# Down projections of three feed-forwards written as seven-product pairs, in four parts instead of three

## The chip, the cores and the metric

The kernel runs on one core of one Trainium2 chip. The metric is the device time of one launch in microseconds (us); the number given for a kernel is the median of its runs. Five engines work side by side, each through its own queue of instructions in order: PE (TensorE: matrix products from SBUF into the eight banks of PSUM), DVE (VectorE), ACT (ScalarE), POOL (GpSimd) and SP (SyncE, which here only issues transfers). POOL also issues transfers, among them all that add to what lies at their destination. An engine waits for another by semaphores.

## The reference, cut to what matters

One step of a streaming encoder of two layers over 512 prompt frames and 64 sample frames, 576 columns in all, with a model width of 1024. Every layer has two feed-forwards, four in the whole, each added with a half:

```
def swiglu(x, w_gu, w_down):
    gate, up = jnp.split(x @ w_gu, 2, axis=-1)
    return (jax.nn.silu(gate) * up) @ w_down
...
x = x + 0.5 * swiglu(rms_norm(x, ln_ffn1[l]), w_ffn1_gu[l], w_ffn1_down[l])
```

The hidden width is 2816, which is 22 tiles of 128. `x @ w_gu` is the gate-up projection, the product with `w_down` the down projection. Between the feed-forwards stand attention, a short convolution, a state space layer and cross attention, which the change leaves alone.

## The kernel before, in words

The activations lie transposed: `X` holds the residual as 8 row tiles (numbered `f`) of 128 x 576. All products are made to nearly fp32 precision from two terms: an operand is split into a high part (`wh`, `xh`, `hh`, rounded by ACT, `hi`) and a low part (`wl`, `xl`, `hl`, the difference, by DVE, `lo`), and a product takes three passes, high by high, high by low and low by high. The 576 columns are two halves of 288 (`HF`), `one` and `two`, so that a product of one 128 x 128 weight tile with all columns costs 6 matmuls of 288 columns.

Three of the four feed-forwards (the second of layer 0, both of layer 1) have `pairs` set. There the gate-up projection goes tile by tile, each hidden tile with its gate and its up weights as one `Pair`: two output tiles, two halves of the inner dimension (4 row tiles each) and two halves of the columns form a 2 x 2 by 2 x 2 product, computed with seven products instead of eight (Strassen's scheme in Winograd's form). A product is 4 row tiles by three passes, 12 matmuls of 288 columns, so a pair is 84 matmuls. Its price lies elsewhere:

* Sums of weights. A pair loads its two weight tiles by SP into `wraw` (`r1`) and `raw2` (`r2`), and `pair_ahead` and `pair_sums` make the four sums that the products need: three transfers issued by POOL that add to their destination (L292 into `raw2`, L300 into `wraw` from DRAM, L302 into `wraw` from `ss`) and one addition on DVE (L299, `ss`). L300 may start only when `ss` has been made and product 0's weights have been split, L302 only when product 2's weights have been split, and product 5's weights (`r1`, second half) exist only when L302 has landed. L292 belongs to the pair after.
* Splits. Each product's weights are split on their own, 128 x 512: one ACT instruction, then one DVE instruction.
* Sums of results. `pair_epi` combines the products, which accumulate in three PSUM banks `T`, `Y`, `W` of the pair (products 0, 3, 4, 6 in `T`; 1 and 5 in `Y`; 2 in `W`); two pairs in turn use six banks. It ends with the hidden tile `td` and its split into `hh` and `hl`.

The order is written out by hand. `pair_steps` sorts the products by `7 * n + at[k]`: a pair's products go 0, 1, 2, 3, then product 6 of the pair before, then 5, 4. `run_steps` emits, ahead of the step in hand, the splits of weights up to four products further on, then the matmuls, then the pair's epilogue, then what was deferred. Since each engine runs its queue in order, on DVE the split of product 5 stands ahead of the splits of product 4 and of the next pair's 0, 1 and 2.

The 22 hidden tiles go in `PARTS` of 6, 8 and 8. After the gate-up pairs of a part (`pair_steps` is called once a part; in its last pair the order is 5, 4, 6 with nothing between), the part's down projection runs in eight steps `down`, one for each `f`: `nj` weight tiles of 6 matmuls each into two PSUM banks, weights loaded and split whole (128 x 768 or 128 x 1024). In the first two parts two DVE instructions (L664, L665) scale the sum by the row statistics `R` and add it to `X`; in the last part `R` has been put into `td` before (L608), and one instruction (L661) adds to `X`. In that part `finalize` follows for each `f`: it prepares the next stage's operands. Where the next stage is again a feed-forward in pairs (after the second feed-forward of layer 0) this is `finalize_s` with its sums and differences `eh`, `el`; after the third one, where the output follows, the last part's down runs as `down_two` and `down_final` in column blocks of 320 and 256.

Of the kernel before, what the change touches and what calls it, by code (L numbers as in the profile page):

```python
# [17 lines left out]
KT = 8  # L18
# [5 lines left out]
NJ = 22  # L24
PARTS = ((0, 6), (6, 8), (14, 8))
PAIRED = (0, 4, 1, 5, 2, 6, 3, 7)
PAST = 256
# [22 lines left out]
class Part:  # L50


    def __init__(self, pair, k):
        self.pair, self.k = pair, k
# [16 lines left out]
class Pair:  # L71

    def __init__(self, g1, g2):
        self.g = (g1, g2)
        self.kw = g1.shape[1] // 2
        self.half = slice(0, self.kw), slice(self.kw, 2 * self.kw)


class Kernel:
# [39 lines left out]
    def operand(self, st):  # L121
        st["hh"] = self.hhl.tile([128, KT, NT], F32R, tag="hh", name="hh")
        st["hl"] = self.hhl.tile([128, KT, NT], F32R, tag="hl", name="hl")

# [178 lines left out]

    def pair_steps(self, grans, ops, epi, late):

        mm = self.nc.tensor.matmul
        todo = []
        for n, (g1, g2) in enumerate(grans):  # L310
            pr = Pair(g1, g2)
            pr.n = n
            pr.banks = [self.banks[:, 3 * (n % 2) + b, :HF] for b in range(3)]
            at = {0: 0, 1: 1, 2: 2, 3: 3, 5: 5, 4: 6, 6: 11}
            if late and n < 2:
                at = ({0: 0, 1: 1, 2: 4, 3: 6, 5: 7, 4: 9, 6: 12}, {0: -5, 1: -4, 2: -2, 3: 1, 5: 3, 4: 4, 6: 6})[n]
            elif n == len(grans) - 1:
                at = {0: 0, 1: 1, 2: 2, 3: 3, 5: 5, 4: 6, 6: 9}
            todo += [(7 * n + at[k], k, pr) for k in range(7)]

        def one(w, k, pr):
            out = pr.banks[PLACE[k]]
            xh, xl = ops()[k]
            for kk in range(4):
                ws = slice(kk * 128, kk * 128 + 128)
                for pi, (ww, xx) in enumerate(((w[0], xh), (w[0], xl), (w[1], xh))):
                    mm(out, ww[:, ws], xx[:, kk], start=k < 3 and kk == 0 and pi == 0, stop=kk == 3 and pi == 2,  # L327
                       skip_group_check=True)
            epi(k, pr)
# [207 lines left out]
    def ffn(self, gu, dn, gain_next, pairs=True, early=False):  # L537
# [3 lines left out]

        def pair_epi(k, pr, first, last, scaled):

            T, Y, W = pr.banks
            tt = V.tensor_tensor
            jj = pr.n
            one, two = slice(0, HF), slice(HF, NT)
            if k == 0:
                if jj == 0:
                    self.operand(st)  # L550
                pr.tb, pr.ta, pr.tc = (self.tmp(n) for n in ("tb", "ta", "tc"))
                self.hi(pr.tb[:, one], T)
# [30 lines left out]
            elif k == 4:  # L583
                tt(pr.tc[:, two], T, pr.tb[:, two], op=ALU.add)  # L584
            else:
                h = self.tmp("td")
                hh, hl = st["hh"][:, jj], st["hl"][:, jj]

                def rest():
                    self.lo(hl, h, hh)  # L590

                def tail():
                    self.hi(hh, h)
                    self.defer(rest, 1)

                if last:
                    for c, u in ((one, T), (two, pr.tc[:, two])):
                        tt(h[:, c], u, pr.ta[:, c], op=ALU.mult)
                        if scaled:
                            tt(h[:, c], h[:, c], st["R"][:, c], op=ALU.mult)  # L600
# [4 lines left out]
                tt(h[:, one], T, pr.ta[:, one], op=ALU.mult)  # L605
                tt(h[:, two], pr.tc[:, two], pr.ta[:, two], op=ALU.mult)
                if scaled:
# [4 lines left out]
        for pi, (j0, nj) in enumerate(PARTS):  # L612
            def lead(wg, wu):
# [55 lines left out]
            def down_mm(w, ps, c0, n, ks):  # L669
                for k in ks:  # L670
                    for pi, (ww, xx) in enumerate(((w[0], st["hh"]), (w[0], st["hl"]), (w[1], st["hh"]))):
                        nc.tensor.matmul(ps, ww[:, k * 128:(k + 1) * 128], xx[:, k, c0:c0 + n],  # L672
                                         start=k == 0 and pi == 0, stop=k == KT - 1 and pi == 2)

# [7 lines left out]
            def down_two(w0, w1, *part):  # L682
                c0, n, _ = part
                ps = [self.ps("ps_d")[:, 0, :n] for _ in range(2)]
                for ks in (range(KT - 1), (KT - 1,)):
                    for e, w in enumerate((w0, w1)):
                        down_mm(w, ps[e], c0, n, ks)
                for e, w in enumerate((w0, w1)):
                    st["w", e] = w
                    down_out(ps[e], e, *part)  # L690

            def down_final(w, f, *part):
                w = st.setdefault(("w", f), w)
                c0, n, _ = part
                ps = self.ps("ps_d")[:, 0, :n]
                down_mm(w, ps, c0, n, range(KT))
                down_out(ps, f, *part)

            if pairs:
                self.pair_steps([(gu[2 * j], gu[2 * j + 1]) for j in range(j0, j0 + nj)], ops,  # L700
                                lambda k, pr, j0=j0, nj=nj: pair_epi(k, pr, j0 + pr.n == 0, pr.n == nj - 1, j0 == PARTS[2][0]),
                                pi == 0)
            for jj in range(0 if pairs else nj):
# [5 lines left out]
                self.step(lambda w, jj=jj: up(w, jj), gu[2 * j + 1])  # L709
            if pairs and pi == 2 and not getattr(gain_next, "pairs", False):  # L710
                self.step(self.fs_close)
            if pi == 2 and gain_next is None:
                def dest(f):
# [17 lines left out]
            for i, f in enumerate(self.order(gain_next)):  # L731
                self.step(lambda w, f=f, nj=nj, la=(pi == 2), fi=(f == 0): down(w, f, nj, la, fi),
                          dn[f, :, j0 * 128:(j0 + nj) * 128])
                if pi == 2 and early and i == 0:
                    self.step(lambda: self.s5_open())
                elif pi == 2 and early and i in HALVES:
                    self.step(lambda *_: None, self.mem_half(1, HALVES.index(i)))
# [1548 lines left out]
def host_arrays(i):  # L2286
# [23 lines left out]
    for n in ("1", "2"):  # L2310
        out["gu" + n] = gu(f(f"w_ffn{n}_gu"))
        out["dn" + n] = np.stack([cols(w) for w in f(f"w_ffn{n}_down")])

    for n in ("xq", "xk", "xo"):
# [83 lines left out]
```

## Time and profile before

| | |
|---|---|
| median of 3 runs | 2562.05 us (2559.88 to 2564.67) |
| profiled execution, its own time | 2562.18 us |
| its span, first to last instruction | 2560.1 us |
| busy: PE, DVE, ACT, POOL | 97%, 64%, 42%, 20% of the span |
| mean granted clock of PE | 0.989 |
| first pair product of the three feed-forwards in pairs | 920 us, 1328 us, 2136 us after the start |

A profile row gives the start of a group, the time it took, the engine, the line of the program, the operation and its operands (output, arrow, inputs), and in brackets how long the engine had been idle before it and which instruction released it. Matmuls overlap, so the time from one start to the next counts, not the length of one.

### The profile page before, as it was taken

The numbers are of one execution on the slowest core, as the hardware profiler recorded it, in microseconds if no ns is written. First come the engines' busy times: TensorE is split into PE (matmuls) and PEld (weight loads), VectorE is DVE, ScalarE is ACT, GpSimd is POOL, SyncE is SP. The second block draws the span as 40 slices with busy tenths as digits, with TensorE's granted clock in tenths as the row PEclk, the third lists the DMA queues.
The fourth block names the chain that finished last, engine by engine and source line by source line (L and its number), as shares of the span: only waits on it lengthen the run. The fifth ranks groups of instructions, "written<-read, shape, count | busy, mean of one in ns | idle before, by whom it ended". The sixth has DMA issues, their size and how long they took to land. (4 is left out here: it accounts for less than half of the span.)

```text
span 2560.1 us, 45526 instructions
## 1 busy us (share of the span) xinstructions
PE 2477.1 (97%) x18499; PEld 2438.1 (95%) x18499; DVE 1628.7 (64%) x2762; ACT 1066.3 (42%) x1847; POOL 524.1 (20%) x667
## 2 busy tenths in 40 slices
PE   8999999999999999999999999999999999999998
PEld 8998999999899999999998999999999999999998
DVE  6645658567775675665776674755753467666574
ACT  5222222325654453443554352542453455344353
POOL 1476245202310010211101110212311001021111
PEclk9999999999999999999999999999999999999999
DMA  4465643321143354645545564745872225464551
GB/s 154 89 188 188 150 116 121 121 85 34 40 140 124 104 133 120 153 115 140 132 112 118 142 141 112 160 138 167 296 238 84 83 95 131 122 157 107 137 136 62
DMA packets 141074, 331.91 MB, mean 130 GB/s; under 512 B 19472, under 2 KB 48320, under 8 KB 140224
## 3 DMA queue, kind: packets, MB, share of 16 engines
q1 hardware_dynamic: 112352, 277.08, 33.8%
q0 software_dynamic: 28512, 51.92, 12.7%
q8 instruction: 145, 2.38, 0.4%
q14 instruction: 65, 0.53, 0.1%
HBM read 279.68 MB, written 31.97 MB: 122 GB/s over the span
## 5 line engine op out<-in xcount | busy, mean ns | idle before, releaser
L141 ACT ACTIVATE wh<-wraw 128x512 fp32r<-128x512 f32 (+2 forms) x543 | 430.3, 803 | 506.5 <-PE banks L406 229.7
L223 DVE TENSOR_TENSOR wl<-wraw,wh 128x1024 fp32r<-128x1024 f32 (+2 forms) x264 | 322.4, 1224 | 168.6 <-ACT wh L141 166.4
L406 PE MATMUL banks<-hh,wh 128*128 128x288 f32 x1768 | 382.4, 298 | 2.8 <-ACT hh L141 2.0
L406 PE MATMUL banks<-hh,wl 128*128 128x288 f32 x1768 | 380.5, 297 | 4.0 <-DVE wl L223 4.0
L406 PE MATMUL banks<-hl,wh 128*128 128x288 f32 x1768 | 380.9, 297 | 0.5 <-DVE hl L147 0.5
L327 PE MATMUL banks<-xh,wh 128*128 128x288 f32 x1056 | 312.0, 295 | 1.3 <-ACT tb L141 0.8
L327 PE MATMUL banks<-xh,wl 128*128 128x288 f32 x1056 | 311.4, 295 | 0.0
L327 PE MATMUL banks<-xl,wh 128*128 128x288 f32 x1056 | 310.9, 294 | 0.0
L406 PEld LDWEIGHTS banks<-hh,wh 128*128 128x128 f32 x1768 | 288.2, 191 | 4.4 <-ACT hh L141 2.5
L406 PEld LDWEIGHTS banks<-hh,wl 128*128 128x128 f32 x1768 | 287.1, 190 | 4.5 <-DVE wl L223 4.5
L406 PEld LDWEIGHTS banks<-hl,wh 128*128 128x128 f32 x1768 | 287.6, 191 | 1.0 <-DVE hl L147 1.0
L406 PE MATMUL banks<-xh,wh 128*128 128x288 f32 x1232 | 267.6, 299 | 10.0 <-ACT wh L141 9.1
L327 PE MATMUL banks<-eh,wh 128*128 128x288 f32 x792 | 238.8, 302 | 37.2 <-DVE tc L584 35.5
L147 DVE TENSOR_TENSOR wl<-wraw,wh 128x512 fp32r<-128x512 f32 x264 | 181.4, 688 | 144.9 <-ACT wh L141 131.7
L406 PE MATMUL banks<-xh,wl 128*128 128x288 f32 x1232 | 265.5, 297 | 5.3 <-DVE wl L223 5.3
L406 PE MATMUL banks<-xl,wh 128*128 128x288 f32 x1232 | 264.3, 296 | 0.0
L327 PE MATMUL banks<-el,wh 128*128 128x288 f32 x792 | 237.6, 300 | 0.0
L327 PE MATMUL banks<-eh,wl 128*128 128x288 f32 x792 | 237.3, 300 | 0.0
L406 PEld LDWEIGHTS banks<-xh,wh 128*128 128x128 f32 x1232 | 199.2, 190 | 12.2 <-ACT wh L141 9.6
L406 PEld LDWEIGHTS banks<-xh,wl 128*128 128x128 f32 x1232 | 199.0, 189 | 7.1 <-DVE wl L223 7.0
L327 PEld LDWEIGHTS banks<-xh,wh 128*128 128x128 f32 x1056 | 198.4, 188 | 2.6 <-DVE td L605 1.4
L406 PEld LDWEIGHTS banks<-xl,wh 128*128 128x128 f32 x1232 | 199.4, 190 | 0.0
(538 smaller groups left out, 4900.5 us busy)
## 6 DMA issues: line engine op xcount, KB each, us to landing
wraw<-in_gu SPq DMA_DIRECT2D x110, 512.0 KB
raw<-in_gu SPq DMA_DIRECT2D x66, 512.0 KB
wraw<-in_dn SPq DMA_DIRECT2D x64, 512.0 KB
raw<-in_gu POOLq DMA_DIRECT2D x66, 256.0 KB, 5.5
wraw<-in_gu POOLq DMA_DIRECT2D x66, 256.0 KB, 4.1
wraw<-ss POOLq DMA_DIRECT2D x66, 256.0 KB, 4.5
wraw<-in_dn SPq DMA_DIRECT2D x32, 384.0 KB
wraw<-in_win SPq DMA_DIRECT2D x17, 512.0 KB
```

What stands on the lines that cost most here:

```text
L141: self.nc.scalar.activation(out, in_, AF.Copy)
L147: self.nc.vector.tensor_tensor(out, in_, hi.bitcast(F32), op=ALU.subtract)
L223: self.lo_engine.tensor_tensor(l[:p, :n], t[:p, :n], h[:p, :n].bitcast(F32), op=ALU.subtract)
L327: mm(out, ww[:, ws], xx[:, kk], start=k < 3 and kk == 0 and pi == 0, stop=kk == 3 and pi == 2, skip_group_check=True)
L406: mm(ps[:M, h, :n], ww[:, k * M:(k + 1) * M], xx[:, k0 + k, h * n:(h + 1) * n], start=first and k == 0 and pi == 0, stop=last and k == kt ...
```

## The change

The gate-up pairs stay. In the three feed-forwards in pairs the 22 tiles are cut into parts of 6, 6, 6 and 4 (`PARTS_S`). In the three parts of 6 the down projection is made in pairs too: output tiles `f` and `f + 4` are the two outputs, the even and the odd tiles of the part the two halves of the inner dimension, the column halves as before. A down pair is seven products of 3 row tiles by three passes, 9 matmuls, 63 in all, and there are four of them a part. The hidden tiles of such a part are scaled by `R` at once and split in the combinations that the seven products need (`q` slots in `hh`, `hl` and new tiles `qeh`, `qel`; `hk` and `hu` keep an even tile and a sum). The down epilogue `down_epi` adds each product to `X` with one DVE instruction. On the host the tiles of the down weights are put in the order `KORDER`. The last part of 4 tiles goes as the last part did before.

All gate-up pairs and down pairs of a feed-forward stand in one sequence, sorted by one call of `pair_steps`; the first gate-up pair of the next part goes ahead of the four down pairs, and its split is held back (`held`) until the last of them. In the sequence's last pair the order is now 4, 5, 6.

```diff
+PARTS_S = ((0, 6), (6, 6), (12, 6), (18, 4))
+KORDER = [j0 + j for j0 in (0, 6, 12) for j in (0, 2, 4, 1, 3, 5)] + [18, 19, 20, 21]
...
-            elif n == len(grans) - 1:
-                at = {0: 0, 1: 1, 2: 2, 3: 3, 5: 5, 4: 6, 6: 9}
+            elif n == len(pairs) - 1:
+                at = {0: 0, 1: 1, 2: 2, 3: 3, 4: 4.5, 5: 5, 6: 6}
...
-            for kk in range(4):
+            kn = pr.kw // 128
+            for kk in range(kn):
...
                 tt(h[:, one], T, pr.ta[:, one], op=ALU.mult)
                 tt(h[:, two], pr.tc[:, two], pr.ta[:, two], op=ALU.mult)
-                if scaled:
-                    tt(h, h, st["R"], op=ALU.mult)
-                self.defer(tail, 1)
+                tt(h, h, st["R"], op=ALU.mult)
+                if direct:
+                    parts = [(st["hh"][:, jj], st["hl"][:, jj], h, None)]
+                elif jj % 2 == 0:
+                    tt(hk[:, 0], hk[:, 1], hk[:, 2], op=ALU.subtract)
+                    parts = [(qh[:, 0:2, kk], ql[:, 0:2, kk], hk[:, 0:2], None)]
+                else:
+                    t = self.tmp("tb")
+                    tt(t[:, one], h[:, two], hk[:, 2], op=ALU.subtract)
+                    V.scalar_tensor_tensor(t[:, two], t[:, one], -1.0, hk[:, 1], op0=ALU.mult, op1=ALU.subtract)
+                    tt(u, h[:, one], t[:, two], op=ALU.add)
+                    parts = [(qh[:, 2:4, kk], ql[:, 2:4, kk], self.h2(h), None),
+                             (st["qeh"][:, :, kk], st["qel"][:, :, kk], self.h2(t), None),
+                             (qh[:, 4, kk], ql[:, 4, kk], u, -1.0)]
...
+        def down_epi(k, pr, last):
...
+            for e, c, ps in {0: ((0, one, T),), 1: ((1, two, Y),), 2: ((0, one, W),), 3: ((0, two, T),), 5: ((0, two, Y),),
+                             4: ((1, two, T),), 6: ((1, one, T),)}[k]:
+                x = self.X[:, pr.f[e], c]
+                V.scalar_tensor_tensor(x, ps, (-0.5, 0.5)[e], x, op0=ALU.mult, op1=ALU.add)
+            if k == 6 and last:
+                st.pop("held")()
...
+        def down_pair(f, j0, nj):
+            pr = Pair(*(dn[e, :, j0 * 128:(j0 + nj) * 128] for e in (f, f + 4)), lambda k, pr: down_epi(k, pr, f == 3), qs)
...
             if pairs:
-                self.pair_steps([(gu[2 * j], gu[2 * j + 1]) for j in range(j0, j0 + nj)], ops,
-                                lambda k, pr, j0=j0, nj=nj: pair_epi(k, pr, j0 + pr.n == 0, pr.n == nj - 1, j0 == PARTS[2][0]),
-                                pi == 0)
+                for jj in range(1 if pi else 0, nj):
+                    gate_up(j0 + jj, jj, nj, end)
+                if not end:
+                    gate_up(j0 + nj, 0, nj, pi == len(parts) - 2)
+                    for f in range(4):
+                        down_pair(f, j0, nj)
+                    continue
+                self.pair_steps(seq)
```

What this does to the queues is seen at three places. First DVE in a part's down projection, in the first feed-forward in pairs. Before, with `wl` the split of one `f`'s weights, `tc` and `X` the two instructions that add its result:

```order
L223 TENSOR_TENSOR wl<-wraw,wh 128x768
L664 SCALAR_TENSOR_TENSOR tc<-banks,R 128x576
L665 TENSOR_TENSOR X<-X,tc 128x576
L223 TENSOR_TENSOR wl<-wraw,wh 128x768
L664 SCALAR_TENSOR_TENSOR tc<-banks,R 128x576
```

The same engine in the changed kernel, in the middle of the down pairs; the first row is the split of a pair's product 5, the `wl` from `raw_10899` that of the next pair's product 1, the row from `ss` that of its product 3:

```order
L152 TENSOR_TENSOR wl<-wraw,wh 128x384
L648 SCALAR_TENSOR_TENSOR X<-banks,X 128x288
L152 TENSOR_TENSOR wl<-wraw,wh 128x384
L648 SCALAR_TENSOR_TENSOR X<-banks,X 128x288
L152 TENSOR_TENSOR wl<-wraw,wh 128x384
L648 SCALAR_TENSOR_TENSOR X<-banks,X 128x288
L152 TENSOR_TENSOR wl<-raw_10899,wh 128x384
L304 TENSOR_TENSOR ss<-raw_10899,wraw 128x384
L648 SCALAR_TENSOR_TENSOR X<-banks,X 128x288
L152 TENSOR_TENSOR wl<-wraw,wh 128x384
L648 SCALAR_TENSOR_TENSOR X<-banks,X 128x288
L152 TENSOR_TENSOR wl<-ss,wh 128x384
```

Three instructions for an `f` (six for two of them) have become fifteen for a pair of them: seven splits, a sum and one addition to `X` behind each product, between the splits.

Second, POOL's queue of transfers at the same place. L297, L305 and L307 are the lines that were L292, L300 and L302; before, this queue held nothing for the down projection:

```order
L305 DMA wraw<-in_gu 128x512
L307 DMA wraw<-ss 128x512
L297 DMA raw_10629<-in_dn 128x384
L305 DMA wraw<-in_dn 128x384
L307 DMA wraw<-ss 128x384
L297 DMA raw_10761<-in_dn 128x384
```

So each down pair now issues the same three adding transfers as a gate-up pair, of 192 KB each instead of 256 KB.

Third, DVE in a gate-up pair, at product 6. Before, in the first two parts, with `td` the hidden tile, between the sum `ss` and the split of product 2:

```order
L299 TENSOR_TENSOR ss<-raw_10178,wraw 128x512
L605 TENSOR_TENSOR td<-banks,ta 128x288
L606 TENSOR_TENSOR td<-tc,ta 128x288
L147 TENSOR_TENSOR wl<-wraw,wh 128x512
```

Now, for an odd tile of a part:

```order
L304 TENSOR_TENSOR ss<-raw_10362,wraw 128x512
L610 TENSOR_TENSOR td<-banks,ta 128x288
L611 TENSOR_TENSOR td<-tc,ta 128x288
L612 TENSOR_TENSOR td<-td,R 128x576
L620 TENSOR_TENSOR tb<-td,hk 128x288
L621 SCALAR_TENSOR_TENSOR tb<-tb,hk 128x288
L622 TENSOR_TENSOR hu<-td,tb 128x288
L152 TENSOR_TENSOR wl<-wraw,wh 128x512
```

Four instructions more stand ahead of the split of product 2; for an even tile two more, the product with `R` and one subtraction. Behind it, an odd tile has three splits of `td`, `tb` and `hu` instead of one.

More of the change, by code (lines that the diff above doesn't have):

```diff
@@ L540, in ffn, with pair_epi @@
         st = {}
-        def pair_epi(k, pr, first, last, scaled):
+        def pair_epi(k, pr, first, last, direct):
             T, Y, W = pr.banks
             tt = V.tensor_tensor
-            jj = pr.n
+            jj = pr.jj
             one, two = slice(0, HF), slice(HF, NT)
             if k == 0:
-                if jj == 0:
+                if first:
                     self.operand(st)
+                    for n, m in (("hk", 3), ("hu", 1)):
+                        st[n] = self.fs["x"].tile([128, m, HF], F32, tag=n, name=n)
+                    for n in ("qeh", "qel"):
+                        st[n] = self.fs["x"].tile([128, 2, 3, HF], F32R, tag=n, name=n)
                 pr.tb, pr.ta, pr.tc = (self.tmp(n) for n in ("tb", "ta", "tc"))
@@ new lines, in rest, with tail @@
+                def rest():
+                    for oh, ol, x, c in parts:
+                        self.lo(ol, x, oh, scale=c)
+                def tail():
+                    for oh, ol, x, c in parts:
+                        self.hi(oh, x, scale=c)
+                    self.defer(rest, 1)
+                if jj == 0 and not first:
+                    st["held"] = tail
+                else:
+                    self.defer(tail, 1)
+        def down_epi(k, pr, last):
+            T, Y, W = pr.banks
+            one, two = slice(0, HF), slice(HF, NT)
+            for e, c, ps in {0: ((0, one, T),), 1: ((1, two, Y),), 2: ((0, one, W),), 3: ((0, two, T),), 5: ((0, two, Y),),
[4 more added lines that the diff above has]
+                st.pop("held")()
@@ L613, in lead @@
+        def down_pair(f, j0, nj):
+            pr = Pair(*(dn[e, :, j0 * 128:(j0 + nj) * 128] for e in (f, f + 4)), lambda k, pr: down_epi(k, pr, f == 3), qs)
+            pr.f = (f, f + 4)
+            seq.append(pr)
+        parts = PARTS_S if pairs else PARTS
+        for pi, (j0, nj) in enumerate(parts):
+            end = pi == len(parts) - 1
             def lead(wg, wu):
@@ L684, in down_two @@
                 ps = [self.ps("ps_d")[:, 0, :n] for _ in range(2)]
-                for ks in (range(KT - 1), (KT - 1,)):
+                for ks in (range(nj - 1), (nj - 1,)):
                     for e, w in enumerate((w0, w1)):
@@ L709, in ffn @@
                 self.step(lambda w, jj=jj: up(w, jj), gu[2 * j + 1])
-            if pairs and pi == 2 and not getattr(gain_next, "pairs", False):
+            if pairs and end and not getattr(gain_next, "pairs", False):
                 self.step(self.fs_close)
-            if pi == 2 and gain_next is None:
+            if end and gain_next is None:
                 def dest(f):
@@ L2312, in host_arrays @@
         out["dn" + n] = np.stack([cols(w) for w in f(f"w_ffn{n}_down")])
+        for l in range(2):
+            if (int(n), l) in LAYERS_S:
+                w = out["dn" + n][l].reshape(8, 128, NJ, 128)
+                out["dn" + n][l] = w[:, :, KORDER].reshape(8, 128, NJ * 128)
     for n in ("xq", "xk", "xo"):
```

66 lines of the change are left out of this document (37 added, 29 removed).

## The prediction

> **What bounds the kernel now.** The page comes first, for the share of PE, then the chain of waits, for the pace of matmuls that wait for nothing.
>
> ```profile
> span 2560.1 us, 45526 instructions
> PE 2477.1 (97%) x18499; PEld 2438.1 (95%) x18499; DVE 1628.7 (64%) x2762; ACT 1066.3 (42%) x1847; POOL 524.1 (20%) x667
> ...
> 1918.44 76.82 PE banks L406 x576
> ...
> 2398.33 82.69 PE banks L327 x624
> ```
>
> PE is busy for 97% of the span: time is matmuls times pace, plus few pauses. The pace is 76.82 / 576 = 0.1334 us, and 82.69 / 624 = 0.1325 us in pair products. A gate-up product of 12 matmuls thus takes 1.59 us and a pair of 84 takes 11.13 us; a down pair of 63 would take 8.35 us. The pauses are in PE's waits and its timeline:
>
> ```profile
> PE banks L327 <- DVE tc L584: 35.5, 12, 4.3
> ...
> 945.09 0.37 PE L327 MATMUL banks<-eh,wh 128*128 128x288 f32 x1 [0.47 <-DVE tc L584]
> ...
> 2160.62 0.37 PE L327 MATMUL banks<-eh,wh 128*128 128x288 f32 x1 [0.47 <-DVE tc L584]
> ...
> 2342.63 0.61 PE L327 MATMUL banks<-eh,wh 128*128 128x288 f32 x1 [3.44 <-DVE tc L584]
> 2343.04 0.44 PE L327 MATMUL banks<-el,wh 128*128 128x288 f32 x1
> 2343.28 0.44 PE L327 MATMUL banks<-eh,wl 128*128 128x288 f32 x1
> ```
>
> Of twelve waits for `tc`, three are the 0.47 us at a feed-forward's start (first and last of three shown); the other nine are the nine ends of parts, (35.5 - 1.4) / 9 = 3.8 us each: the last pair's product 6 must wait until DVE has read product 4's bank. Behind such a pause matmuls start every 0.24 us for a while, at half the clock. By windows (columns: stretch, length, busy time of PE, PEld, DVE, ACT, POOL, granted clock, DMA):
>
> ```profile
> 990.00:1000.00 10.00, 6.44 (x38) 6.21 (x38) 5.42 (x12) 3.53 (x6) 0.00 (x0) 0.85 0.35 108
> 1000.00:1010.00 10.00, 10.00 (x76) 10.00 (x75) 4.97 (x7) 1.69 (x2) 0.00 (x0) 0.98 0.27 79
> 1122.00:1132.00 10.00, 6.61 (x50) 6.38 (x50) 5.60 (x12) 3.53 (x6) 0.00 (x0) 1.00 0.39 120
> ...
> 2280.00:2290.00 10.00, 10.00 (x78) 10.00 (x77) 7.65 (x15) 5.52 (x11) 2.65 (x3) 1.00 0.72 175
> ```
>
> The clock costs 10 x 0.15 + 10 x 0.02 = 1.7 us at the first end and nothing at the second. The last row is the steady gate-up stage: PE without a gap, DVE 7.65 of 10. That looks like room, but the question is what DVE waits for. One turn of the preparation of weights, rows of POOL, ACT and DVE put in order of time:
>
> ```profile
> 2292.80 0.86 POOL L300 DMA_DIRECT2D wraw<-in_gu  x1 [8.25 <-DVE td L605]
> 2293.90 0.87 POOL L302 DMA_DIRECT2D wraw<-ss  x1 [0.24 <-DVE ta L573]
> ...
> 2289.91 0.41 ACT L141 ACTIVATE tc<-banks 128x288 f32<-128x288 f32 x1 [0.56 <-PE banks L327]
> 2299.09 0.63 ACT L141 ACTIVATE wh<-wraw 128x512 fp32r<-128x512 f32 x1 [2.40 <-DMA wraw<-ss]
> ...
> 2299.76 1.51 DVE L147 TENSOR_TENSOR wl<-wraw,wh 128x512 fp32r<-128x512 f32 x2 [2.46 <-ACT wh L141]
> 2301.18 0.45 DVE L556 TENSOR_TENSOR ta<-banks,tb 128x288 f32<-128x288 f32 x1
> 2301.55 0.68 DVE L147 TENSOR_TENSOR wl<-wraw,wh 128x512 fp32r<-128x512 f32 x1
> 2302.15 0.68 DVE L147 TENSOR_TENSOR wl<-raw,wh 128x512 fp32r<-128x512 f32 x1
> 2302.76 0.68 DVE L299 TENSOR_TENSOR ss<-raw,wraw 128x512 f32<-128x512 f32 x1
> ...
> 2304.09 0.68 DVE L147 TENSOR_TENSOR wl<-wraw,wh 128x512 fp32r<-128x512 f32 x1
> ...
> 2304.08 0.87 POOL L300 DMA_DIRECT2D wraw<-in_gu  x1 [8.40 <-DVE td L605]
> 2305.18 0.86 POOL L302 DMA_DIRECT2D wraw<-ss  x1 [0.23 <-DVE ta L573]
> ```
>
> This is a **closed ring**: L300 and L302 of one pair, landing (6.29 us from L300's start to ACT), 0.67 to DVE's split of product 5, then without a gap splits and `ss` until 2303.44 (3.68), 0.64 to the next L300: 11.28 us, against PE's 11.13. DVE's 2.46 us of idle time are inside the ring and not free. A ring longer than PE's turn eats the lead of the splits and then stops PE before product 5 in every pair, however idle all engines look. The lead is small: ACT, which had waited for it, read product 3's bank at 2289.91, so the next pair's product 3 ends 11.13 later, at 2301.0; one product of 1.59 us follows, product 5 starts at 2302.6, and its split ended at 2300.4. That is 2.2 us.
>
> **The change part by part.** The sum is made against the profiled execution, 2562.2 us (span 2560.1 and 2.1 around it), which is the median of the runs.
>
> Matmuls: a feed-forward's down was 22 x 48 = 1056, and is 12 pairs x 63 + 4 x 48 = 948. Three times 108 at 0.1334 us: **-43**.
>
> Ends of parts: six of nine go, since products of the next pair now stand where PE paused: 6 x 3.8 = 23, and 1.7 for clock at four or five of them: **-30**. At the three that remain, product 5 (1.59 us) stands between 4 and 6: **-5**. The Trainium skill ("TensorE: Matmul & The Clock Gate", Part 1) has the clock halved only after an idle window of 3.4 us; by that the remaining pauses of 2.2 us would lose their slow stretch also, another 5 us, and the pause of the 1122 window, which kept its clock, shows that the windows are not tied to the pause.
>
> The ring in the down pairs: the widths are 384 and 192 KB. A split of 384 is worked out from rows of two widths:
>
> ```profile
> 1005.35 0.95 DVE L223 TENSOR_TENSOR wl<-wraw,wh 128x768 fp32r<-128x768 f32 x1
> ```
>
> 0.95 at 768 against 0.68 at 512; the step from 2301.55 to 2302.15 is 0.60, so 0.60 - 0.14 = 0.46 at 384. The additions to `X` read a bank and 288 columns as L556 does, step 0.37. From the split of product 5 to `ss` DVE has four splits, `ss` and three additions: 5 x 0.46 + 3 x 0.37 + 0.1 = 3.5. ACT to DVE 0.56, `ss` to L300 0.64. Landing is shown for 256 KB only:
>
> ```profile
> raw<-in_gu POOLq DMA_DIRECT2D x66, 256.0 KB, 5.5
> wraw<-in_gu POOLq DMA_DIRECT2D x66, 256.0 KB, 4.1
> ```
>
> The last figures are medians from an issue to its own landing; the ring has two issues in a row. Upper end: as now, 5.9 (6.29 here, 5.5 in the rows below). Lower end: L302 lands 1.6 us sooner when L300 is not right ahead (3.6 below against 5.19), so most of the time grows with two transfers in a row; if all of that is bytes, a quarter off each gives 4.7. I take 5.2, between them. Ring: 3.5 + 0.56 + 0.64 + 5.2 = 9.9 against 8.35, so 1.55 lost a pair, times 36: **+56** (38 to 82). That needs no further engine to be full. The Trainium skill ("DMA: Bandwidth & Descriptors", Anatomy of one DMA) fits a transfer issued by POOL with 2.0 us fixed and 436 KB per us after; by it 64 KB less saves 0.15 us a transfer, and the upper end would be near. The medians above, 4.1 and 5.5 us, lie well over the 2.6 us of that fit, so it doesn't decide here.
>
> The ring in the gate-up pairs: the last part of before, where `td` is multiplied by `R` ahead of product 2's split, is the nearest row:
>
> ```profile
> 2424.22 1.51 DVE L147 TENSOR_TENSOR wl<-wraw,wh 128x512 fp32r<-128x512 f32 x2 [1.79 <-ACT wh L141]
> 2434.70 1.51 DVE L147 TENSOR_TENSOR wl<-wraw,wh 128x512 fp32r<-128x512 f32 x2 [0.88 <-ACT wh L141]
> ...
> 2428.54 0.88 POOL L300 DMA_DIRECT2D wraw<-in_gu  x1 [7.75 <-DVE td L605]
> 2430.43 0.88 POOL L302 DMA_DIRECT2D wraw<-ss  x1 [1.01 <-DVE ta L573]
> 2452.43 0.86 POOL L302 DMA_DIRECT2D wraw<-ss  x1 [1.03 <-DVE ta L573]
> ...
> 2434.04 0.63 ACT L141 ACTIVATE wh<-wraw 128x512 fp32r<-128x512 f32 x1 [1.31 <-DMA wraw<-ss]
> 2456.97 0.63 ACT L141 ACTIVATE wh<-wraw 128x512 fp32r<-128x512 f32 x1 [2.25 <-DMA wraw<-ss]
> ```
>
> A ring of 10.48 us with a landing of 3.6; others land in 4.5, which makes 11.4. Ahead of product 2's split an even tile adds 0.37, an odd tile 1.2: means 11.25 and 12.15 by the two landings, 0.1 to 1.0 over PE's turn. I take 0.35, nearer to the short landing, because L302 now starts still later behind L300. Times 54 pairs: **+19** (5 to 30). The odd tile's two extra splits fall into DVE's wait and are covered; if that cover goes, they cost 1.1 us each odd pair. The lead of 2.2 us is spent once a feed-forward and not won back.
>
> The last part's down in the second feed-forward of layer 0: PE now takes 3.2 us an `f` instead of 6.4, while DVE's work for the next operands stays:
>
> ```profile
> 1308.55 0.76 DVE L661 SCALAR_TENSOR_TENSOR X<-banks,X 128x576 f32<-128x576 f32 x1 [0.47 <-PE banks L406]
> 1311.64 0.76 DVE L384 TENSOR_TENSOR acc<-acc,sq 128x576 f32<-128x576 f32 x1 [0.72 <-ACT sq L383]
> ...
> 1314.95 0.76 DVE L661 SCALAR_TENSOR_TENSOR X<-banks,X 128x576 f32<-128x576 f32 x1 [1.13 <-PE banks L406]
> 1319.66 0.69 DVE L147 TENSOR_TENSOR wl<-wraw,wh 128x512 fp32r<-128x512 f32 x1
> ```
>
> 3.8 us for an `f` under 4, 4.7 for the others, and 0.6 for each split: 9.7 us for two against 6.4 of PE. Four times 3.3 is **+13**, the clock behind the pause within it. The other two last parts have no such sums to make, so between nothing and half of that for both: **+3** (0 to 7).
>
> Sum: -43 - 30 - 5 + 56 + 19 + 13 + 3 = +13, so 2575 us.
>
> **The rivals.** (1) The forecast, rings over PE's turn, with 4.8 to 5.6 us for the landing and 0.15 to 0.5 for the gate-up turn: 2553 to 2596.
>
> (2) The landing shrinks with the bytes, to 4.3: ring 9.0, down +24, gate-up +7, sum -31: **2531**. It is the side of faster, and decides from a landing of 4.8 us on, where the losses (42 and 19) equal the other terms' 62. For it: L302 alone takes 3.6 us at full size. Against it: in the down pairs L302 follows L300 closely again.
>
> (3) The landing doesn't shrink: 5.9, ring 10.6, down +82, gate-up +27, sum +47: **2609**. For it: 5.5 and 6.29 in the rows, where nothing shows bytes as the cause. The fit of the Trainium skill named above would have it nearly so.
>
> (4) PE stays the bound throughout, because the ring's parts overlap in a way that the rows don't show: sum -62, **2500**. Against it: 4.7 us of the ring are instructions in a queue, and the landing would have to be 3.6.
>
> That the matmuls don't go is excluded by the order of instructions.
>
> **How the numbers follow.** Chances: (1) 0.47, (2) 0.27, (3) 0.20, (4) 0.06. The likeliest gives 2575. The range 2518 to 2612 leaves out (4), the lower edge of (2) and the upper half of (3), under 2 in 10. By 0.2%, which is about what a measurement of this kernel can tell from no change (5 us): faster is (2), (4) and an edge of (1), 0.36; same 0.10; slower 0.54.
>
> **What would show it.** PE's waits should have the `tc` wait at three ends instead of nine, and a new wait of about 1.5 us in each down pair, before product 5, for `wh` or `wl` or for an addition to `X` queued behind it. L305 should recur every 9.9 us in the down pairs and not every 8.35; ACT's wait for `wraw<-ss` should be over 2 us in each. PE should stand still for about 10 us before the second feed-forward in pairs begins. If L305 recurs every 8.4 us with PE full, the ring was wrong and (4) holds; if the landing is under 4.8 us, (2).

## The result, and the profile after

| | before | after |
|---|---|---|
| median | 2562.5 us (2559.88 to 2564.67) | 2641.4 us (2636.9 to 2646.6) |
| ratio, 95% interval | 1 | 1.0309 (1.0286 to 1.0332) |
| span of the profiled execution | 2560.1 us | 2637.5 us |
| mean granted clock | 0.989 | 0.979 |

The change makes the kernel 3.1% slower, 79 us. The forecast was 2575 us: the side was right, but 2641 lies above the range, which ended at 2612.

The page of after opens as follows, and its waits of PE (us in total, times, longest) stand below it:

```profile
span 2637.5 us, 46458 instructions
PE 2485.6 (94%) x18175; PEld 2422.4 (92%) x18175; DVE 1828.0 (69%) x3350; ACT 1148.7 (44%) x2099; POOL 620.1 (24%) x775
...
PE banks L331 <- DVE X L648: 56.2, 36, 4.1
PE banks L331 <- DVE hl L152: 22.8, 9, 3.2
PE banks L331 <- ACT tb L146: 10.1, 22, 1.1
...
PE banks L331 <- DVE tc L592: 1.4, 3, 0.5
```

The 324 matmuls are gone (18499 to 18175), and so are the waits for `tc`: 35.5 us before, 1.4 now, the three at the starts of the feed-forwards. In their place stand two larger ones: 56.2 us for additions to `X`, and 22.8 us for `hl`, nine times, once at the start of each part's down pairs. PE is busy 8.5 us longer with fewer matmuls, in part because more of them run at half the clock: by the trace's clock records 109 us of the span against 58 before.

By phases of PE (first matmul of one kind to first of the next, summed over the three feed-forwards):

| phase | at PE's pace | measured | lost beyond pace | forecast for the change |
|---|---|---|---|---|
| matmuls of the downs | -45 | -45 | | -43 |
| gate-up, before | 734.6 | 798.7 | 64.1 | |
| gate-up, after | 734.6 | 789.2 | 54.6, so **-9.5** | -35 + 19 = -16 |
| down pairs, after | 300.5 | 417.0 | **+116.5** | +56 |
| other downs, before | 422.6 | 442.5 | 19.9 | |
| last parts' downs, after | 76.8 | 116.0 | 39.2, so **+19.3** | +13 + 3 = +16 |

(Pace: 0.1325 us a matmul in pairs, 0.1334 in whole downs.) The sum is +81; the spans differ by 77.4, and the other stages hold the rest. One line is far off: the 36 down pairs lose 116.5 us and not 56.

The two lines with -9.5 and +19.3 have to be read together. The first gate-up pair of the second feed-forward in pairs takes 18.11 us where it took 11.11, because the last part before it, now of 4 tiles, leaves less time for the operands (experiment 4, with such parts alone, has 18.12). These 7.0 us stand in the gate-up line but belong to the last parts, which so cost about +26 and not 16. Without them the gate-up phases gain 16.5, as was forecast.

The turn of the ring in one part of the first feed-forward, rows of POOL, ACT, DVE and SP of after. L305 and L307 are the lines L300 and L302 of before; L290 is SP's load of a later pair's second weights into `raw2`:

```profile
1003.55 0.89 POOL L305 DMA_DIRECT2D wraw<-in_dn  x1 [7.84 <-DVE td L610]
1015.67 0.86 POOL L305 DMA_DIRECT2D wraw<-in_dn  x1 [7.12 <-DVE ss L304]
1027.52 0.86 POOL L305 DMA_DIRECT2D wraw<-in_dn  x1 [6.31 <-ACT wh L146]
1039.54 0.87 POOL L305 DMA_DIRECT2D wraw<-in_dn  x1 [9.36 <-ACT wh L146]
1040.16 1.14 POOL L307 DMA_DIRECT2D wraw<-ss  x1
1052.72 0.87 POOL L305 DMA_DIRECT2D wraw<-in_gu  x1 [10.50 <-DVE X L648]
...
1047.60 1.45 ACT L146 ACTIVATE wh<-wraw 128x384 fp32r<-128x384 f32 x3 [7.64 <-DMA wraw<-ss]
...
1035.37 0.56 DVE L152 TENSOR_TENSOR wl<-wraw,wh 128x384 fp32r<-128x384 f32 x1 [5.63 <-ACT wh L146]
1048.15 0.56 DVE L152 TENSOR_TENSOR wl<-wraw,wh 128x384 fp32r<-128x384 f32 x1 [5.86 <-ACT wh L146]
...
1041.59 0.33 SPq L290 DMA_DIRECT2D raw<-in_gu  x1
```

The ring is the one that was forecast: L305 and L307 together, a landing that ACT waits for, DVE's split of product 5, then rows of DVE up to the next L305. From the split at 1035.37 to L305 at 1039.54 it takes 4.17 us (forecast 3.5 + 0.64 = 4.14), and from ACT's start to DVE's 0.55. But from L305 at 1039.54 to ACT at 1047.60 the landing takes **8.06 us**, where 5.2 was taken and 5.9 was the upper end: the turn is 12.78 us instead of 9.9. In the middle of this landing SP issues L290, here 512 KB for a gate-up pair two places on (384 KB where the later pair is a down pair). It follows L307 each time, because it waits for the split of product 6 out of the buffer that it overwrites. The trace's DMA packets show the two side by side. While SP's packets ran, in the third and fourth turns of all nine parts, POOL's queue moved 84 KB per us; in the same landings without them it moved 141. The load does no such harm where L307 doesn't follow closely behind L305: earlier in this part L307 went out 3.75 us after L305 and ACT took it up 3.37 us later, though SP issued its load 1.29 us behind it. Most of L307's packets had gone when the load's first one came, at 1022.1.

```profile
1019.42 0.88 POOL L307 DMA_DIRECT2D wraw<-ss  x1 [2.88 <-DVE X L648]
...
1022.79 1.35 ACT L146 ACTIVATE wh<-wraw 128x384 fp32r<-128x384 f32 x3 [4.31 <-DMA wraw<-ss]
...
1020.71 0.33 SPq L290 DMA_DIRECT2D raw<-in_dn  x1
```

Over all nine parts, the four turns from one L305 to the next behind a down pair's own take on average 12.11, 10.95, 12.21 and 12.78 us (36 turns, mean 12.0). By the order they hold 25 products of 9 matmuls and 3 of 12, 34.6 us at PE's pace against 48.05: 13.5 us a part, about 121 in nine, which is the 116.5 above seen from POOL. The 54 gate-up turns, reckoned the same way, are 16.7 us over PE's pace in all; 9.3 of it lie in the nine first ones behind the down pairs (11.77 us on average against 10.73), and the others are 0.14 to 0.26 us over.

The first of the four turns has another cause. DVE's rows from 999.63 to 1015.03 stand one behind the other with 0.43 us between them: the odd tile's end (its products, the row factor, three sums, three low parts) falls together with the next tile's sums, `ss` and the first additions to `X`. By windows (length, busy time of PE, PEld, DVE, ACT, POOL, granted clock, DMA):

```profile
1000.00:1010.00 10.00, 7.19 (x50) 6.57 (x49) 9.27 (x20) 5.42 (x12) 2.65 (x3) 0.97 0.44 85
1010.00:1020.00 10.00, 9.40 (x52) 9.40 (x53) 8.53 (x19) 3.08 (x7) 1.44 (x2) 0.69 0.49 115
...
1030.00:1040.00 10.00, 7.16 (x43) 6.95 (x42) 4.63 (x11) 3.11 (x7) 0.64 (x2) 0.83 0.60 151
1040.00:1050.00 10.00, 7.34 (x55) 7.14 (x55) 3.80 (x10) 2.40 (x5) 2.22 (x3) 1.00 0.59 120
```

In the first two rows DVE is busy for 17.8 of 20 us; in the last two PE, DVE, ACT and POOL are all far from full, which is what a ring looks like. The clock column shows the price behind the pauses, 0.69 and 0.83.

### The profile page after: what moved, and what is told of

Read it like the earlier page. It is cut to its first block, busy times and chain, and to the rows that moved or that the text cites. A ratio compares the mean times of both kernels' runs of the same rounds, so it can differ in the third digit from the quotient of the medians.

```text
span 2637.5 us, 46458 instructions
## 1 busy us (share of the span) xinstructions
PE 2485.6 (94%) x18175; PEld 2422.4 (92%) x18175; DVE 1828.0 (69%) x3350; ACT 1148.7 (44%) x2099; POOL 620.1 (24%) x775
## 3 DMA queue, kind: packets, MB, share of 16 engines
q0 software_dynamic: 44064, 73.16, 17.4%
## 5 line engine op out<-in xcount | busy, mean ns | idle before, releaser
L146 ACT ACTIVATE wh<-wraw 128x512 fp32r<-128x512 f32 (+3 forms) x639 | 441.7, 713 | 446.3 <-DMA wraw<-ss 304.9
L152 DVE TENSOR_TENSOR wl<-wraw,wh 128x512 fp32r<-128x512 f32 (+1 forms) x408 | 259.1, 638 | 244.1 <-ACT wh L146 236.3
L228 DVE TENSOR_TENSOR wl<-wraw,wh 128x1024 fp32r<-128x1024 f32 (+2 forms) x216 | 260.6, 1211 | 146.1 <-ACT wh L146 143.8
L410 PE MATMUL banks<-hl,wh 128*128 128x288 f32 x968 | 210.0, 299 | 5.7 <-DVE hl L152 5.7
L331 PE MATMUL banks<-hh,wh 128*128 128x288 f32 x540 | 165.1, 306 | 52.2 <-DVE X L648 51.9
L410 PE MATMUL banks<-hh,wh 128*128 128x288 f32 x968 | 210.8, 300 | 3.5 <-ACT hh L146 1.7
L410 PE MATMUL banks<-hh,wl 128*128 128x288 f32 x968 | 209.6, 298 | 3.4 <-DVE wl L228 3.4
L410 PEld LDWEIGHTS banks<-xh,wl 128*128 128x128 f32 x1232 | 200.6, 191 | 6.6 <-DVE wl L228 6.6
L331 PEld LDWEIGHTS banks<-xh,wl 128*128 128x128 f32 x1056 | 199.3, 189 | 3.2 <-DVE wl L152 2.3
L410 PEld LDWEIGHTS banks<-xl,wh 128*128 128x128 f32 x1232 | 200.3, 190 | 0.0
L331 PEld LDWEIGHTS banks<-xl,wh 128*128 128x128 f32 x1056 | 199.6, 189 | 0.3 <-DVE xl L154 0.3
```

The source lines that it names most:

```text
L146: self.nc.scalar.activation(out, in_, AF.Copy)
L152: self.nc.vector.tensor_tensor(out, in_, hi.bitcast(F32), op=ALU.subtract)
L228: self.lo_engine.tensor_tensor(l[:p, :n], t[:p, :n], h[:p, :n].bitcast(F32), op=ALU.subtract)
L410: mm(ps[:M, h, :n], ww[:, k * M:(k + 1) * M], xx[:, k0 + k, h * n:(h + 1) * n], start=first and k == 0 and pi == 0, stop=last and k == kt ...
```

## The experiments

Theory at the start: the down ring costs what it costs because SP's load collides with L307's landing. The rival: other terms (cutting into four parts, the wait for `hl`, the gate-up turn) make the loss.

**1. Open the ring.** In the down pairs L307 isn't issued, so the weights of product 5 lack the sum.

```diff
-        elif k == 2:
+        elif k == 2 and pr.kw == 512:
             self.nc.gpsimd.dma_start(pr.r1[:, two], pr.src[3], accum_op=ALU.add)
```

> Leaves out the transfer that adds ss to the second half of r1 (L302 in the kernel before) in the 36 down pairs, so product 5 of a down pair is made with weights that lack the sum, and its split waits for no landing. Theory A (the ring: that landing holds up DVE's queue, and with it the additions to X that PE waits for): the waits for X in the down pairs (56 us in the changed kernel) go, most of the half-clock stretches with them (about 15 us), so about 2565 us, L305 every 8.4 to 9.5 us in the down pairs. Rival B (DVE's own work in the down stage is the limit, or the late splits of the odd tile): 2630 us or more, with the waits for X still there.

Measured 2587.0 us, ratio 1.0082 (1.0060 to 1.0105): by the ratios 2.3% or 58 us less than the change, where about 76 us had been expected. The `X` waits fall to 14.0 us, the `hl` waits stay (24.1). The ring in the down pairs is the largest loss, but not the only one. The down pairs here take 353.6 us, still 53 over pace. Their turns are 12.11, 8.76, 9.02 and 10.56 us: the first is untouched.

**2. Take the collision away.** The loads into `raw2` go through POOL's queue, behind the transfers that add.

```diff
-        self.nc.sync.dma_start(pr.r2[:, :n], pr.g[1])
+        self.nc.gpsimd.dma_start(pr.r2[:, :n], pr.g[1])
```

> The second weight tile of every pair is loaded by POOL's queue and no longer by SP's, so that it lines up behind the adding transfers in the same queue. Theory C (in the down pairs the landing of ss grew to 6.7 to 7.4 us because SP's load of the next raw2 tile is let go by the split of product 6, 0.9 us after that transfer was issued, and shares the 16 DMA engines with it): the landing falls to about 4.5 us, the turn of the ring from 12.4 to about 10 us, 2585 to 2605 us. Rival D (transfers of 192 KB that add are slow by themselves or behind one another): landing stays at 6 to 7 us, 2641 us or more, as POOL has 100 issues more.

Measured 2603.9 us, ratio 1.0134 (1.0113 to 1.0156): 1.75%, 45 us less than the change, with no work taken out. Of these, 42 lie in the down pairs (374.6 us against 417.0). Rows of POOL and ACT of this kernel, same place in the program:

```profile
1031.77 0.88 POOL L305 DMA_DIRECT2D wraw<-in_dn  x1 [5.51 <-ACT wh L146]
1032.39 1.14 POOL L307 DMA_DIRECT2D wraw<-ss  x1
...
1034.04 0.95 POOL L290 DMA_DIRECT2D raw<-in_gu  x1
1041.97 0.88 POOL L305 DMA_DIRECT2D wraw<-in_dn  x1 [6.98 <-ACT wh L146]
...
1037.25 1.35 ACT L146 ACTIVATE wh<-wraw 128x384 fp32r<-128x384 f32 x3 [4.99 <-DMA wraw<-ss]
```

L305 to ACT is 5.48 us and the turn 10.20: without the collision the forecast's 5.2 and 9.9 nearly hold. The medians of the second addition, from issue to landing, after and then here:

```profile
wraw<-ss POOLq DMA_DIRECT2D x66, 256.0 KB, 3.5
...
wraw<-ss POOLq DMA_DIRECT2D x36, 192.0 KB, 4.9
```

```profile
wraw<-ss POOLq DMA_DIRECT2D x66, 256.0 KB, 3.4
...
wraw<-ss POOLq DMA_DIRECT2D x36, 192.0 KB, 4.1
```

In the change a transfer of 192 KB lands 1.4 us later than one of 256 KB. Without the load beside it the gap is 0.7 us and does not vanish, for in half of the down pairs L307 still goes out 0.62 us behind L305. The bytes alone didn't set the landing; what ran ahead of it and beside it counted more.

**3. Give the ring time.** Product 5 of a down pair goes behind the next pair's four products.

```diff
+            elif pr.kw == 384:
+                at = {0: 0, 1: 1, 2: 2, 3: 3, 5: 10.5, 4: 6, 6: 11}
```

> Only the order: in a down pair product 5 goes after the next pair's product 3 and just ahead of its own product 6 (at 10.5 instead of 5). Theory A: the next pair's second transfer is issued before this pair's product 5 is split, the ring is open, the landing is hidden behind four more products: 2570 to 2590 us, no wait for X over 1 us in the down pairs. Rival B (DVE's own work): 2630 us or more.

Measured 2625.1 us, ratio 1.0227 (1.0201 to 1.0253): 0.8% less than the change, but a miss of what was expected. Rows of ACT, POOL and SP show what became the last instead:

```profile
1032.51 0.53 ACT L146 ACTIVATE wh<-raw 128x384 fp32r<-128x384 f32 x1 [3.34 <-DMA raw<-in_dn]
1038.61 1.05 ACT L146 ACTIVATE wh<-wraw 128x384 fp32r<-128x384 f32 x2 [3.13 <-DMA wraw<-in_dn]
1044.66 0.63 ACT L146 ACTIVATE wh<-raw 128x512 fp32r<-128x512 f32 x1 [5.00 <-DMA raw<-in_gu]
...
1035.95 1.46 POOL L297 DMA_DIRECT2D raw<-in_gu  x1
...
1036.62 0.33 SPq L289 DMA_DIRECT2D wraw<-in_gu  x1
```

ACT now waits for `raw<-in_dn` and `raw<-in_gu`. By the times of landing these are L297's additions for the next pair's product 1, which stand behind L307 in POOL's queue; the one of 1035.95 landed 8.55 us after its issue. With product 5 later, `wraw` comes free later too, and SP's load L289 goes out 1.9 to 2.3 us behind L305, where in the change it went out 2.75 us ahead of it. Now both of SP's loads fall beside POOL's transfers. The ring was opened at one landing and closed at the next.

**4. The cut alone.** The kernel before, its downs as they were, but in parts of 6, 6, 6 and 4.

```diff
+PARTS_S = ((0, 6), (6, 6), (12, 6), (18, 4))
...
-        for pi, (j0, nj) in enumerate(PARTS):
+        parts = PARTS_S if pairs else PARTS
+        for pi, (j0, nj) in enumerate(parts):
+            end = pi == len(parts) - 1
```

> The kernel before with parts of 6, 6, 6 and 4 and its old down projections: the cut into four parts alone. If ends of parts cost what the profile of before shows (3.8 us of pause and up to 1.7 us of clock), three more ends give +17 us, and the last part of the second feed-forward of layer 0, with half the matmuls for the same work of DVE, about +13 us: 2585 to 2600 us. Rival (the end of a part is hidden and the last part keeps up): 2562 to 2570 us.

Measured 2596.2 us, ratio 1.0123 (1.0099 to 1.0147), +30 us. By phases of PE the downs take 19.4 us more and the gate-up phases 14.0 us more. The first, and 7.0 of the second in the first pair of the second feed-forward in pairs, are the price of last parts with 4 tiles, which the change pays as well. The 7 us that are left go with three more ends: the waits for `tc` are 37.6 us in 14 where they were 35.5 in 12, so that an end is a little shorter here, and the clock is 0.984.

**5 and 6. Is the wait for `hl` a loss of its own?** The last odd tile's product 6 goes ahead, first with products 4 and 5 exchanged (alone, with experiment 2, and with experiment 1), then in their old order.

```diff
+            elif pr.odd:
+                at = {0: 0, 1: 1, 2: 2, 3: 3, 4: 4.5, 5: 5, 6: 8.5}
...
+            pr.odd = jj == 5 and not direct
```

> The last odd tile of each part (nine in all) issues its product 6 behind two products of the next tile instead of four (its product 4 moves ahead of its product 5), so that DVE makes the operands of the down pairs some 3.2 us sooner. Theory A (the waits of 2.5 us for hl at the start of each down are set by how late that tile is finished, and they bring the half clock behind them): the hl waits fall from 22.8 us to under 5, and with some clock the ratio goes from 1.031 to 1.018-1.024 (2609-2624 us). Rival B (DVE's backlog sets the start of the down pairs, so a tile finished sooner only puts the wait elsewhere, on X or wh): hl falls, X or other waits rise by as much, and the ratio stays at 1.028-1.034.

> The edit of the earlier run that loads r2 through POOL's queue, and the early product 6 of the last odd tile, together. Theory A (two separate losses: the collision of transfers in the ring, 1.75%, and the operands at the start of each down, 0.7-1.3%): they add, ratio 1.000-1.007 (2563-2580 us). Rival B (with one of them gone the other is hidden by the lead of the splits, or the wait moves): ratio 1.010-1.016.

> The down pairs' second addition by DMA left out (part of the sums of the down weights is missing), and the early product 6 of the last odd tile. What is left here is the change without its ring in the down pairs and without the wait at their start. If the other terms of the prediction hold (matmuls -43, ends -35, gate-up ring +19, end of the second feed-forward +13, other ends +3: -43 together) the ratio should be 0.983 (2522 us, 2510-2540). If it stays above 0.995, a further loss that the prediction has not named, or gains of the ends that were too large, make up the rest.

Measured 1.0398 (1.0370 to 1.0425), 1.0242 (1.0220 to 1.0265) and 1.0125 (1.0104 to 1.0146), all three slower than without the edit (1.0309, 1.0134 and 1.0082; of the last two kernels the intervals just touch). The third was to show whether the prediction's other terms hold without the ring, 0.983. Neither it nor experiment 1 comes near: experiment 1 ends some 64 us above, of which 53 are what its down pairs still lose. The second form:

```diff
+            elif pr.odd:
+                at = {0: 0, 1: 1, 2: 2, 3: 3, 5: 5, 4: 6, 6: 9}
```

> The last odd tile's products keep their order (5, then 4), and only its product 6 moves ahead, from behind four products of the next tile to behind two; nothing is put in front of ACT's read of product 3's bank, which cost 31.4 us in the earlier try. Theory A (the hl waits are a loss of their own, 22.8 us with half clock behind): hl under 6 us, a short wait for tc of under 1 us nine times, ratio 1.019-1.024. Rival B (the rings of the down pairs set the end of each down, and the hl wait only takes from the waits behind it): hl falls, the X waits grow from 56.2 us to over 70, ratio 1.027-1.032.

> r2 loaded through POOL's queue and the same early product 6. Theory A: both losses gone, ratio 1.002-1.008. Rival B: the ring of 10.2 us that is left still sets each down's length, X waits grow from 25.7 us to over 40, ratio 1.010-1.014.

Measured 1.0427 (1.0399 to 1.0455) and, with experiment 2, 1.0236 (1.0206 to 1.0266), again slower. In both forms the `hl` waits at the starts of the down pairs are gone, and others have come; PE's waits and ACT's rows of the second form:

```profile
PE banks L334 <- DVE X L651: 57.5, 48, 3.4
PE banks L334 <- ACT tc L147: 30.5, 9, 3.5
PE banks L334 <- ACT tb L147: 20.7, 30, 1.8
...
1003.47 0.68 ACT L147 ACTIVATE hh<-td 128x576 fp32r<-128x576 f32 x1 [1.87 <-DVE td L615]
1004.45 0.68 ACT L147 ACTIVATE qeh<-tb 128x576 fp32r<-128x576 f32 x1 [0.30 <-DVE tb L624]
1005.04 0.42 ACT L149 ACTIVATE hh<-hu 128x288 fp32r<-128x288 f32 x1
...
1005.79 0.39 ACT L147 ACTIVATE tc<-banks 128x288 f32<-128x288 f32 x1
```

The odd tile's high parts (`hh`, `qeh`, `hh`) have moved ahead of ACT's read of product 3's bank (`tc<-banks`). They wait for DVE, the read stands behind them, and product 4 of the next tile waits up to 3.5 us for the read, nine times. So these five kernels don't answer the question; they say what a place in a queue is worth.

**7. The same question, on DVE alone.** The three low parts of that tile come directly behind the high ones, ahead of four rows of other work; ACT's queue and PE's order stay.

```diff
-                    self.defer(rest, 1)
+                    rest() if jj == 5 and not direct else self.defer(rest, 1)
```

> Only DVE's order is edited: the three splits hl, qel, hl of the last odd tile of each part come right behind their rounded halves, ahead of four rows of other work (two splits of weights, the read of product 4's bank, one addition to X; about 2.3 us). ACT's queue and PE's order stay. Theory A (the hl wait of 2.5 us nine times is a loss of its own): hl falls from 22.8 us to under 5, part of the half clock behind it goes too, ratio 1.019-1.025. Rival B (the turn of the ring, 12 us in the down pairs, sets the end of each down; PE then only waits later): X rises from 56.2 us by 10 or more, ratio 1.027-1.032.

> The same order on DVE, and r2 loaded through POOL's queue, with which the ring's turn was 10.2 us. Theory A: ratio 1.001-1.008. Rival B: X rises from 25.7 us to over 40, ratio 1.010-1.014.

Measured 1.0339 (1.0305 to 1.0374), and with experiment 2's load 1.0148 (1.0128 to 1.0168): no gain in either; the intervals overlap those without the edit. PE's waits of the first:

```profile
PE banks L331 <- DVE X L648: 55.5, 41, 3.3
PE banks L331 <- ACT wh L146: 17.4, 8, 2.4
...
PE banks L331 <- DVE hl L152: 3.5, 7, 0.9
```

Of 22.8 us for `hl` 3.5 are left, and 17.4 us for `wh` have come. The rival holds in substance, though not on `X`: PE waits at another product of the same turn. That turn, the first of a down, is 11.81 us on average against 12.11, but the second is 11.74 against 10.95, so that the four together are no shorter. Moving rows inside the turn only moved the wait. That DVE's amount of work sets this turn is read from its rows; no run took the work itself away.

**8. The gain without the change.** The kernel before with one line edited: at each end of a part the last pair's product 4 goes ahead of its product 5, as the change has it in its one last pair.

```diff
-                at = {0: 0, 1: 1, 2: 2, 3: 3, 5: 5, 4: 6, 6: 9}
+                at = {0: 0, 1: 1, 2: 2, 3: 3, 4: 4.5, 5: 5, 6: 6}
```

> The kernel before, with one edit: at each end of a part the last pair's product 4 goes ahead of its product 5, as in the change, so that product 5 (1.59 us) stands between the bank's read and product 6. The prediction's term for it is 1.6 us an end, -5 us for three ends; here there are nine: -14 us, with the half clock that falls away at some of them -14 to -20, ratio 0.992-0.995. Rival: product 4 then waits for ACT's read of product 3's bank as in the earlier try (3.5 us), ratio 1.002-1.007.

Measured **2521.8 us** (2520.1 to 2527.0), ratio **0.9812** (0.9789 to 0.9836): the fastest kernel of the study, and far more than expected. PE's waits for `tc` are 1.4 us instead of 35.5, the clock is 0.993 instead of 0.989. The gate-up phases take 754.6 us instead of 798.7, 44 us less: 34.1 of it are the waits, and the rest agrees with less half clock (34 us of the span instead of 58). The profiled spans differ by 35.2 us only, since this profiled execution took 9 us more elsewhere and was the slowest of its kernel's four (2527.0); the medians, measured beside each other, differ by 46.7 (before 2568.5 there). DVE's rows at the first end of a part say why, of the kernel before:

```profile
991.29 0.45 DVE L573 TENSOR_TENSOR ta<-banks,tc 128x288 f32<-128x288 f32 x1
991.77 0.46 DVE L568 TENSOR_TENSOR ta<-ta,R 128x288 f32<-128x288 f32 x1
994.28 0.96 DVE L223 TENSOR_TENSOR wl<-wraw,wh 128x768 fp32r<-128x768 f32 x1 [2.06 <-ACT wh L141]
995.16 0.45 DVE L584 TENSOR_TENSOR tc<-banks,tb 128x288 f32<-128x288 f32 x1
```

and of this one:

```profile
992.19 0.45 DVE L584 TENSOR_TENSOR tc<-banks,tb 128x288 f32<-128x288 f32 x1
993.75 0.96 DVE L223 TENSOR_TENSOR wl<-wraw,wh 128x768 fp32r<-128x768 f32 x1 [1.12 <-ACT wh L141]
994.63 0.45 DVE L573 TENSOR_TENSOR ta<-banks,tc 128x288 f32<-128x288 f32 x1
```

L584 is the read of product 4's bank for which PE waits. Before, it stood in DVE's queue behind a split (L223) that itself waited 2.06 us for ACT. With product 4 one place earlier it runs ahead of that split, and PE also has product 5 to do meanwhile.

## Why the prediction was right in its side and wrong in its size

**Right:** the bound (PE), the 324 matmuls, the six ends whose `tc` wait goes, the ring as the mechanism that takes more than the matmuls give, its place (POOL, ACT and DVE rows as listed), DVE's part of it (4.17 us against 4.14), and the ring in the gate-up pairs (+16.7 us by POOL's turns against +19). The working of that last term has a slip that did no harm: 0.1 to 1.0 us a turn in 54 turns is 5 to 54, and not 5 to 30. The last parts were under-reckoned by 10 us (+26 against +16).

**Wrong, the failed step:** the term "ring in the down pairs, +56 (38 to 82)", measured as +116.5. It was mis-sized in three ways:

* *Landing.* The forecast took 5.2 us, on the reasoning that fewer bytes land sooner. In the third and fourth turns, where L307 follows L305 closely, it was 6.7 to 8.5 us, on average 7.49 and 7.66, because a load of 512 KB that SP issues meanwhile slows POOL's transfers. The rows of before could not show this, since there the load came 2.75 us behind L302 and not 1.43; but that the shorter turn moves SP's load towards the landing could have been worked out from the order. Removing the collision (experiment 2) is worth 45 us. It brings the third turn within 0.3 us of the forecast's value; the second and fourth stay at 10.67 and 10.70.
* *First turn of a down.* The forecast counted every pair's turn as the same ring, and let the odd tile's extra work fall into DVE's wait. At the last odd tile there is no such wait. The turn is 12.11 us where PE needs 8.75 by the order (6 products of 9 matmuls and one of 12): 3.4 us, about 30 us in nine. That DVE's work sets it is read from its rows and not shown by a run. This is the forecast's own caveat, "if that cover goes, they cost 1.1 us each odd pair", at nine places and three times the size.
* *Clock.* The price of a pause was counted at the ends of parts but not in the ring. The mean granted clock fell from 0.989 to 0.979, which on 2485 us of PE is some 25 us; it is contained in the numbers above.

With a ring near the forecast's for turns two to four (experiment 2: 31.56 us in three turns, 25.85 at pace, 51 us in nine parts), 39 for the collision (35.94 against 31.56) and 30 for the first turns, the down pairs come to 121, against 116.5 measured by PE's rows.

**Rivals.** (3), "the landing doesn't shrink", named the right quantity but ended at 5.9. That a landing can also become longer than at full size was left out, so that what came true lay above every rival. (2) and (4) fell with the landing; (2)'s threshold of 4.8 us isn't reached even without the collision (5.48).

**Ends of parts.** "-5" for the three last ends rested on product 5's 1.59 us alone. Experiment 8 shows that the exchange removes the whole wait, since it also changes the place in DVE's queue. In the change the waits for `tc` fell by 34.1 us, where the ends were forecast at -35 with the clock. With +16.7 for the gate-up turns and 7.0 from the last part this comes to -10.4, against the -9.5 measured. PE also waits 10.1 us for `tb` there (2.5 before), reads that stand in ACT's queue behind waits for `wraw<-ss`.

**What would show it.** The wait for `tc` at three ends "instead of nine" was too careful: there is none left at any end. L305 recurs every 12.0 us in the down pairs and not every 9.9. Before the second feed-forward in pairs PE stands still for 7.7 us between the start of the last part's downs and the end of that feed-forward's first pair, where about 10 were forecast. The waits in each down pair came as forecast but longer: 2.84 us at 1036.45 and 2.65 at 1049.22, and they are named `X` because the addition stands behind the late split in DVE's queue. Experiment 1, with the same additions and no landing, has 14.0 us of them left.

## What to carry to other kernels

Before work is taken off a busy engine, find the closed ring of transfers and small instructions beside it and measure its turn: when the engine's own turn becomes shorter than the ring, the gain is gone, and a shorter turn also pushes other transfers into the ring's landing. Look for the instruction that the bound engine waits for in its own engine's queue: what stands ahead of it there, and what that waits for. Here one exchange in the order of products gave 1.9%, more than all the matmuls that the change removed (45 of 2562 us, 1.8%), and without its cost.

## What the runs showed of the hardware

Half the clock came behind pauses of under 3 us, and not behind every longer one. PE's rows of after:

```profile
1046.28 0.29 PE L331 MATMUL banks<-hh,wl 128*128 128x288 f32 x1
1049.22 0.38 PE L331 MATMUL banks<-hh,wh 128*128 128x288 f32 x1 [2.65 <-DVE X L648]
...
1051.40 0.44 PE L331 MATMUL banks<-qel,wh 128*128 128x288 f32 x1
1051.64 0.44 PE L331 MATMUL banks<-qeh,wl 128*128 128x288 f32 x1
...
1050.00:1052.00 2.00, 1.81 (x9) 1.49 (x9) 2.00 (x5) 0.09 (x1) 0.00 (x0) 0.58 0.71 236
1052.00:1054.00 2.00, 2.00 (x11) 2.00 (x10) 2.00 (x6) 1.16 (x2) 1.28 (x2) 0.57 0.07 27
```

PE stood still for 2.65 us. The first matmuls behind the pause still start 0.13 us apart; the slow stretch, 0.24 us apart, begins 1.1 us later and lasts 3.4 us, which costs 1.7 us.

The clock records of the traces show why it comes late. The clock changes on a fixed grid of 3.41 us, and every stretch at half clock lasts one or two such steps, the one at the kernel's end excepted. What preceded it was a step in which PE was idle for about half or more: from 900 us on, 24 of the 25 drops in after came behind steps with PE busy for 2% to 56% (32% here; the other drop stands at the kernel's end), and steps that kept the clock followed ones with 45% or more. So it is partly luck whether a pause costs clock. In the kernel before, the pause of 3.39 us that ended at 1128.29 fell across two steps, with PE busy for about half of each, and the clock stayed at 1.00.

The Trainium skill ("TensorE: Matmul & The Clock Gate", Part 1) has the clock drop after an idle window of about 3.4 us. The length agrees with the records here; that the window must be idle does not, since 2.65 us of pause were enough.

Transfers of two queues delayed each other. An addition of 192 KB took 4.9 us from issue to landing (median) with SP's load beside it and 4.1 with the load behind it in POOL's queue. In the third turns L305 to ACT went from 7.49 to 5.47 us on average, and POOL's queue moved 84 KB per us while the load's packets ran and 141 while they didn't.
